# Differential attention: where the normalized head outputs are kept, and how many bias tiles there are

## The chip, the cores and the metric

One core of a Trainium2 chip runs one launch of the kernel. The metric is the device time of a launch in microseconds; the times shown are the median of three runs and the time of one further, profiled execution. The core has five engines that run side by side and wait for each other by semaphores: TensorE (PE; its weight loads are shown as PEld), VectorE (DVE), ScalarE (ACT), GpSimd (POOL) and SyncE (SP), which here issues nearly all DMA transfers, in order, from one queue.

## The reference, cut to what matters

The model is a decoder trunk of two layers over 256 tokens of width 2048 in float32. Layer 0 mixes tokens by gated linear attention, layer 1 by differential attention; each is followed by a SwiGLU block. The change lies in layer 1, in the part below, which is done for 8 heads of size 128 with values of size 256:

```
scores = einsum('bhmqd,bhmkd->bhmqk', qb, k_sh)          # m = 0, 1: two score maps per head
scores = scores + bias                                   # T5 bias by distance, one table per head
scores = where(dist >= 0, scores, -inf)
p = softmax(scores, axis=-1)
a = p[:, :, 0] - lam * p[:, :, 1]
o = einsum('bhqk,bhke->bhqe', a, v_sh)
...
o = rmsnorm(o, subln_g) * (1.0 - lambda_init)
return o.reshape(b, s, D_MODEL) @ w_out
```

The queries are taken in two blocks of 128, called b = 0 and b = 1 here. By causality block 0 sees 128 keys and block 1 sees 256.

## The kernel before, in words

Every large product is made from weights that stream through one ring of buffers: SP loads 512 KB of weights into a `raw` tile (line 223, five buffers), ACT casts it to a high part `hi` (line 238, nine buffers), DVE makes the rest `lo` (line 241), and TensorE multiplies with both. A product that wants the result transposed is made in blocks by `block_w` (line 429): 32 matmuls (lines 438, 439) accumulate one PSUM tile `acc`, and its two halves are added by way of a scratch tile: ACT copies one half to it (line 450), DVE adds (line 451). `scratch()` (line 187) gives tiles of 128x512 from one tag `hs` with three buffers.

The stage of the change begins when the keys are made and goes on into the output product. For each head h two blocks of `diff_w_q` give q(h), DVE scales it (line 1121), and `diff_stages` (line 954) is called. It loads the head's bias tile by SP (line 959) and puts six steps on a list with due times; `tick()` counts them down, once in the middle and once at the end of the first half of a block, once in the middle of its second half, and once after each block. One head is eight ticks long. The steps and their ticks:

- 3, `scores`: for each block b, two matmuls of q with the keys (line 968), DVE adds the bias into the score tile s0 or s1 (line 972), DVE takes the maximum (line 976), ACT makes the exponentials in place (line 978).
- 6, `combine`: DVE makes a = p0 - lam p1 in place (lines 985 to 990).
- 9, `a_T`: PE transposes the three 128x128 pieces of a (line 998, one of b = 0 and two of b = 1), ACT copies them to the tile aT (line 1000).
- 11, `att_v`: six matmuls of aT with the values into two acc tiles (line 1007), ACT takes their squares (line 483).
- 13, `normed`: DVE, POOL (line 478) and DVE normalize (line 1019); the result is called og.
- 14, `out_T`: four transposes of og (line 1028), ACT and DVE write the high and low part to diff_oT (lines 1031, 1032).

So the last steps of head h fall into the time of head h+1. In the order of the program `scores` of head h+1 (its tick 3, which is tick 11 of head h) comes before `normed` and `out_T` of head h. Score tiles have one buffer for each b: s1 of head h+1 is written in the place of s1 of head h, and has to wait for the last use of it. Before the change og lies in that place: `normed` writes both blocks' og over s1 of its own head, and `out_T` reads it from there:

```
og = ctx["s"][1][0][:, b, :]
```

After head 7 `proj_out` follows (line 827): the product of diff_oT with `diff_w_out` (lines 302 to 304), in four column chunks; the step s of a chunk needs diff_oT of head s. The steps of heads 6 and 7 that are still due fall into its first chunk.

A planner puts the instructions of each engine in order before the launch: it follows the program's order as priority, plays the program through on times of its own, and takes what is ready. The order that the engines then run is fixed, and each engine takes its instructions in that order.

Of the kernel before, what the change touches and what calls it, by code (L numbers as in the profile page):

```python
# [11 lines left out]
F32 = mybir.dt.float32  # L12
# [6 lines left out]
P = 128  # L19
D = 2048  # L20
SEQ = 256
# [130 lines left out]
class Trunk:  # L152
# [801 lines left out]
    def diff_stages(self, dp, oT, q, kT, v, h):  # L954
        nc = self.nc
        ctx = {}
        bias = dp.tile([P, SEQ], F32, tag="bias", name=f"bias{h}", bufs=2)
        src = self.bias_dram[h]
        nc.sync.dma_start(bias, bass.AP(tensor=src.tensor, offset=src.offset + 127, ap=[[383, P], [1, SEQ]]))

        def scores():
            ctx["s"] = []
            for b in range(2):
                n = P * (b + 1)
                sp = self.acc()
                sp3 = sp[:, : 2 * n].rearrange("p (m k) -> p m k", m=2)
                for m in range(2):
                    nc.tensor.matmul(
                        sp3[:, m, :], q[:, m, b * P : (b + 1) * P], kT[:, 2 * h + m, :n], start=True, stop=True
                    )  # L970
                s = dp.tile([P, 2, n], F32, tag=f"s{b}", name=f"s{h}_{b}")
                nc.vector.tensor_tensor(
                    out=s, in0=sp3, in1=bias[:, None, SEQ - n :].to_broadcast([P, 2, n]), op=ALU.add
                )
                st = self.stat(8)
                nc.vector.tensor_reduce(out=st[:, 0:2], in_=s, axis=AX.X, op=ALU.max, negate=True)
                for m in range(2):
                    nc.scalar.activation(
                        s[:, m, :], s[:, m, :], AF.Exp, bias=st[:, m : m + 1], accum_out=st[:, 2 + m : 3 + m]
                    )  # L980
                ctx["s"].append((s, st))

        def combine():
            for s, st in ctx["s"]:
                nc.vector.reciprocal(st[:, 4:6], st[:, 2:4])
                nc.vector.tensor_tensor(out=st[:, 6:7], in0=st[:, 5:6], in1=self.neg_lam, op=ALU.mult)
                nc.vector.tensor_scalar(
                    out=s[:, 1, :], in0=s[:, 1, :], scalar1=st[:, 6:7], scalar2=None, op0=ALU.mult
                )
                nc.vector.scalar_tensor_tensor(  # L990
                    out=s[:, 0, :], in0=s[:, 0, :], scalar=st[:, 4:5], in1=s[:, 1, :], op0=ALU.mult, op1=ALU.add
                )

        def a_T():
            tpa = self.tp()
            for b, (s, _) in enumerate(ctx["s"]):
                for kb in range(b + 1):
                    nc.tensor.transpose(tpa[:, b + kb, :], s[:, 0, kb * P : (kb + 1) * P], self.ident)
            ctx["aT"] = dp.tile([P, 3, P], F32, tag="aT", name=f"aT{h}")
            nc.scalar.copy(ctx["aT"], tpa[:, :3, :])  # L1000

        def att_v():
            ctx["o"] = []
            for b in range(2):
                o = self.acc()
                for kb in range(b + 1):
                    nc.tensor.matmul(  # L1007
                        o[:, :SEQ], ctx["aT"][:, b + kb, :], v[:, kb, h * SEQ : (h + 1) * SEQ],
                        start=(kb == 0), stop=(kb == b),
                    )  # L1010
                ss = self.stat()
                self.square(o[:, :SEQ], ss[:, 0:1])
                ctx["o"].append((o, ss))

        def normed():
            ctx["og"] = []
            for b, (o, ss) in enumerate(ctx["o"]):
                og = ctx["s"][1][0][:, b, :]
                nc.vector.scalar_tensor_tensor(
                    out=og, in0=o[:, :SEQ], scalar=self.rstd(ss, SEQ, 1), in1=self.subg, op0=ALU.mult, op1=ALU.mult  # L1020
                )
                ctx["og"].append(og)

        def out_T():
            tpo = self.tp()
            for b in range(2):
                for j in range(2):
                    nc.tensor.transpose(tpo[:, 2 * j + b, :], ctx["og"][b][:, j * P : (j + 1) * P], self.ident)
            hi, lo = (oT.part(2 * h, 2, slice(None), i) for i in range(2))
            tpo2 = tpo.rearrange("p (j b) t -> p j (b t)", j=2)  # L1030
            nc.scalar.copy(hi, tpo2)
            nc.vector.tensor_tensor(out=lo, in0=tpo2, in1=hi.bitcast(F32), op=ALU.subtract)

        for subs, fn in ((3, scores), (6, combine), (9, a_T), (11, att_v), (13, normed), (14, out_T)):
            self.defer(subs, fn)
# [201 lines left out]
```

## Time and profile before

| | |
|---|---|
| median of three runs | 2243.23 us (2242.36 to 2243.86) |
| the profiled execution: its time | 2241.63 us |
| its span, first to last instruction | 2239.9 us |
| mean granted TensorE clock | 0.999 of full speed |
| PE, PEld, DVE, ACT busy | 99%, 82%, 72%, 52% of the span |
| DMA | 438 MB, 196 GB/s over the span |
| the stage of the change, from the first `scores` to the last `out_T` | 1318.9 to 1458 us of the span |

The profile is of one execution. A wait is shown with the engine and line that ended it. Times in the rows are microseconds from the first instruction, and durations of a group are nanoseconds of one instruction where the row gives a mean.

### The profile page before, as it was taken

The numbers are of one execution on the slowest core, as the hardware profiler recorded it, in microseconds if no ns is written. First come the engines' busy times: TensorE is split into PE (matmuls) and PEld (weight loads), VectorE is DVE, ScalarE is ACT, GpSimd is POOL, SyncE is SP. The second block draws the span as 40 slices with busy tenths as digits, with TensorE's granted clock in tenths as the row PEclk, the third lists the DMA queues.
The fourth block names the chain that finished last, engine by engine and source line by source line (L and its number), as shares of the span: only waits on it lengthen the run. The fifth ranks groups of instructions, "written<-read, shape, count | busy, mean of one in ns | idle before, by whom it ended". The sixth has DMA issues, their size and how long they took to land.

```text
span 2239.9 us, 28021 instructions
## 1 busy us (share of the span) xinstructions
PE 2210.2 (99%) x10310; PEld 1835.3 (82%) x10310; DVE 1605.4 (72%) x2093; ACT 1166.4 (52%) x1602; POOL 38.9 (2%) x68
## 2 busy tenths in 40 slices
PE   8999999999999999999999999999999999999998
PEld 7887888888888888888788887788888888888886
DVE  7865554986885886787665567649868858867975
ACT  8654444755553554455565455447555535544552
POOL 2000000000000000000000000000000000000000
PEclk9999999999999999999999999999999999999999
DMA  8555555665565556566665554465655655565573
GB/s 299 168 174 180 176 175 188 213 225 198 201 220 181 186 192 223 170 206 258 208 206 179 188 175 147 163 183 209 228 179 197 217 178 197 192 216 172 200 254 103
DMA packets 123135, 438.37 MB, mean 196 GB/s; under 512 B 13883, under 2 KB 16612, under 8 KB 121460
## 3 DMA queue, kind: packets, MB, share of 16 engines
q1 hardware_dynamic: 121964, 434.99, 57.9%
q8 instruction: 81, 1.33, 0.2%
q10 hardware_dynamic: 1032, 1.57, 0.2%
q14 instruction: 58, 0.48, 0.1%
HBM read 428.11 MB, written 9.97 MB: 196 GB/s over the span
## 4 chain that ended last, share of the span: by engine, by line
PE 97%; DVE 1%; ACT 1%; issue 1%; DMA 0%; POOL 0%; SPq 0%; DVEq 0%; POOLq 0%; ACTq 0%
PE acc L304 14%; PE acc L302 14%; PE acc L303 14%; PE acc L347 12%; PE acc L345 12%; PE acc L346 12%; PE acc L438 8%; PE acc L439 4%; PE tp L459 1%; PE tp L494 1%; PE tp L347 1%; PE tp L345 1%; PE tp L346 1%; PE acc L1007 1%; DVE lo L241 0%
## 5 line engine op out<-in xcount | busy, mean ns | idle before, releaser
L241 DVE TENSOR_TENSOR lo<-raw,hi 128x1024 fp32r<-128x1024 f32 x842 | 1013.7, 1223 | 513.1 <-ACT hi L238 509.7
L238 ACT CAST hi<-raw 128x1024 fp32r<-128x1024 f32 x846 | 873.4, 1052 | 830.6 <-PE acc L304 375.5
L346 PE MATMUL acc<-lo,h_ffn 128*128 128x512 f32 x780 | 304.3, 390 | 0.0
L347 PE MATMUL acc<-hi,h_ffn 128*128 128x512 f32 x780 | 304.1, 390 | 0.0
L345 PE MATMUL acc<-hi,h_ffn 128*128 128x512 f32 x780 | 303.9, 390 | 0.0
L302 PE MATMUL acc<-hi,f_ffn_gT 128*128 128x512 f32 x704 | 274.8, 390 | 0.0
L303 PE MATMUL acc<-lo,f_ffn_gT 128*128 128x512 f32 x704 | 274.1, 389 | 0.0
L304 PE MATMUL acc<-hi,f_ffn_gT 128*128 128x512 f32 x704 | 272.1, 389 | 0.0
L345 PEld LDWEIGHTS acc<-hi,h_ffn 128*128 128x128 f32 x780 | 146.4, 188 | 30.5
L347 PEld LDWEIGHTS acc<-hi,h_ffn 128*128 128x128 f32 x780 | 146.5, 188 | 30.4
L346 PEld LDWEIGHTS acc<-lo,h_ffn 128*128 128x128 f32 x780 | 146.5, 188 | 30.2
L302 PEld LDWEIGHTS acc<-hi,f_ffn_gT 128*128 128x128 f32 x704 | 132.2, 188 | 27.8 <-issue 0.6
L304 PEld LDWEIGHTS acc<-hi,f_ffn_gT 128*128 128x128 f32 x704 | 132.2, 188 | 27.4
L303 PEld LDWEIGHTS acc<-lo,f_ffn_gT 128*128 128x128 f32 x704 | 132.2, 188 | 27.1
L302 PE MATMUL acc<-hi,h_mix 128*128 128x512 f32 x256 | 102.1, 400 | 0.0
L347 PE MATMUL acc<-hi,f_ffn_forms 128*128 128x512 f32 x260 | 101.8, 392 | 0.0
L345 PE MATMUL acc<-hi,f_ffn_forms 128*128 128x512 f32 x260 | 101.8, 392 | 0.0
L346 PE MATMUL acc<-lo,f_ffn_forms 128*128 128x512 f32 x260 | 101.2, 389 | 0.0
L303 PE MATMUL acc<-lo,h_mix 128*128 128x512 f32 x256 | 100.3, 392 | 0.0
L304 PE MATMUL acc<-hi,h_mix 128*128 128x512 f32 x256 | 100.1, 392 | 0.0
L438 PE MATMUL acc<-h_mix,hi 128*128 128x512 f32 x272 | 96.7, 400 | 0.0
L438 PE MATMUL acc<-h_q,hi 128*128 128x512 f32 x256 | 93.2, 405 | 0.0
(227 smaller groups left out, 3351.0 us busy)
## 6 DMA issues: line engine op xcount, KB each, us to landing
raw<-in_w_gu_dram SPq DMA_DIRECT2D x352, 512.0 KB, 4.6
raw<-in_w_d_dram SPq DMA_DIRECT2D x176, 512.0 KB, 4.4
raw<-in_gla_w_r_dram SPq DMA_DIRECT2D x32, 512.0 KB, 3.6
raw<-in_gla_w_v_dram SPq DMA_DIRECT2D x32, 512.0 KB, 3.6
raw<-in_gla_w_out_dram SPq DMA_DIRECT2D x32, 512.0 KB, 3.6
raw<-in_w_v_dram SPq DMA_DIRECT2D x32, 512.0 KB, 4.4
raw<-in_w_k_dram SPq DMA_DIRECT2D x32, 512.0 KB, 3.5
raw<-in_diff_w_q_dram SPq DMA_DIRECT2D x32, 512.0 KB, 3.5
```

Source lines behind the costliest of these rows:

```text
L238: nc.scalar.copy(hi, src)
L241: eng.tensor_tensor(out=lo, in0=src, in1=hi.bitcast(F32), op=ALU.subtract)
L302: nc.tensor.matmul(ps, ah, rh, start=(kt == 0), stop=False)
L303: nc.tensor.matmul(ps, ah, rl, start=False, stop=False)
L304: nc.tensor.matmul(ps, al, rh, start=False, stop=(kt == 2 * ns - 1))
L345: nc.tensor.matmul(ps, ah, wh, start=first, stop=False)
L346: nc.tensor.matmul(ps, ah, wl, start=False, stop=False)
L347: nc.tensor.matmul(ps, al, wh, start=False, stop=last)
L438: nc.tensor.matmul(ps, lh, aT.both(kt), start=(kt == 0), stop=False)
L439: nc.tensor.matmul(ps[:, SEQ:], ll, aT.hi(kt), start=False, stop=(kt == KT - 1))
L459: nc.tensor.transpose(tp[:, j, :], src[:, j * P : (j + 1) * P], self.ident)
L494: nc.tensor.transpose(tp[:, j, :], xc[:, j * P : (j + 1) * P], self.ident)
```

## The change

Two lines differ. The bias tile of a head gets the pool's one buffer, where it had two. And og of each block is written to a scratch tile of its own (the first 256 of its 512 columns), where it was written over s1. The number of instructions and their sizes stay the same.

```diff
@@ def diff_stages(self, dp, oT, q, kT, v, h):
-        bias = dp.tile([P, SEQ], F32, tag="bias", name=f"bias{h}", bufs=2)
+        bias = dp.tile([P, SEQ], F32, tag="bias", name=f"bias{h}")
...
         def normed():
             ctx["og"] = []
             for b, (o, ss) in enumerate(ctx["o"]):
-                og = ctx["s"][1][0][:, b, :]
+                og = self.scratch()[:, :SEQ]
                 nc.vector.scalar_tensor_tensor(
                     out=og, in0=o[:, :SEQ], scalar=self.rstd(ss, SEQ, 1), in1=self.subg, op0=ALU.mult, op1=ALU.mult
                 )
```

## Rows read from the trace of the kernel before

**Rows 1.** The page: busy time of each engine, and the chain that ended last, by engine.
```profile
PE 2210.2 (99%) x10310; PEld 1835.3 (82%) x10310; DVE 1605.4 (72%) x2093; ACT 1166.4 (52%) x1602; POOL 38.9 (2%) x68
...
PE 97%; DVE 1%; ACT 1%; issue 1%; DMA 0%; POOL 0%; SPq 0%; DVEq 0%; POOLq 0%; ACTq 0%
```

**Rows 2.** Windows: stretch, length, busy PE, PEld, DVE, ACT, POOL (instructions), clock, DMA share, GB/s.
```profile
1318.86:1332.96 14.10, 14.10 (x84) 12.41 (x83) 10.28 (x20) 9.61 (x19) 0.00 (x0) 1.00 0.55 175
1332.96:1349.16 16.20, 14.87 (x86) 12.78 (x85) 13.17 (x27) 9.10 (x23) 1.06 (x2) 1.00 0.48 157
...
1397.87:1414.17 16.30, 14.98 (x87) 12.87 (x86) 11.64 (x24) 8.52 (x20) 1.09 (x2) 1.00 0.46 138
...
1438.19:1462.00 23.81, 20.27 (x95) 16.27 (x94) 13.28 (x26) 10.36 (x23) 2.19 (x4) 1.00 0.56 199
```

**Rows 3.** Waits from 1305 to 1470 us: who for whom, total us, times, longest.
```profile
ACT hi L238 <- PE acc L438: 37.3, 31, 1.8
...
PE acc L1007 <- ACT aT L1000: 7.9, 6, 1.3
...
PE acc L302 <- ACT diff_oT L1031: 1.2, 1, 1.2
...
PE acc L304 <- DVE diff_oT L1032: 1.1, 1, 1.1
```

**Rows 4.** Timeline of PE: start, duration, line, tiles, count, idle time before.
```profile
1346.00 0.44 PE L998 MATMUL tp<-ident,s 128*128 128x128 f32 x2
1347.76 1.56 PE L1007 MATMUL acc<-v_sh,aT 128*128 128x256 f32 x6 [1.33 <-ACT aT L1000]
...
1353.94 0.38 PE L1028 MATMUL tp<-ident,s 128*128 128x128 f32 x2
```

**Rows 5.** Timeline of ACT over the same head.
```profile
1346.01 1.04 ACT L238 CAST hi<-raw 128x1024 fp32r<-128x1024 f32 x1 [1.72 <-PE acc L438]
1346.96 0.36 ACT L450 COPY hs<-acc 128x256 f32<-128x256 f32 x1
1347.23 0.48 ACT L1000 COPY aT<-tp 128x384 f32<-128x384 f32 x1
...
1357.53 0.36 ACT L450 COPY hs<-acc 128x256 f32<-128x256 f32 x1
```

**Rows 6.** Timeline of DVE over the same head.
```profile
1339.76 0.69 DVE L972 TENSOR_TENSOR s<-acc,bias 128x512 f32<-128x512 f32 x1 [0.33 <-PE tp L1028]
...
1345.47 0.48 DVE L990 SCALAR_TENSOR_TENSOR s<-s,st 128x256 f32<-128x256 f32 x1
...
1351.07 0.47 DVE L1019 SCALAR_TENSOR_TENSOR s<-acc,st,subg 128x256 f32<-128x256 f32 x1
```

**Rows 7.** Timelines of DVE, PE and ACT for head 0.
```profile
1321.76 0.68 DVE L972 TENSOR_TENSOR s<-acc,bias 128x512 f32<-128x512 f32 x1
...
1326.03 0.49 DVE L990 SCALAR_TENSOR_TENSOR s<-s,st 128x256 f32<-128x256 f32 x1
...
1330.27 0.38 PE L998 MATMUL tp<-ident,s 128*128 128x128 f32 x2
...
1331.66 1.46 PE L1007 MATMUL acc<-v_sh,aT 128*128 128x256 f32 x6
...
1330.68 0.48 ACT L1000 COPY aT<-tp 128x384 f32<-128x384 f32 x1 [0.93 <-PE tp L998]
```

**Rows 8.** Timeline of PE at the end of the stage (heads 6 and 7).
```profile
1442.67 0.50 PE L302 MATMUL acc<-hi,diff_oT 128*128 128x512 f32 x1 [1.18 <-ACT diff_oT L1031]
...
1445.05 0.50 PE L304 MATMUL acc<-hi,diff_oT 128*128 128x512 f32 x1 [1.07 <-DVE diff_oT L1032]
...
1448.68 1.56 PE L1007 MATMUL acc<-v_sh,aT 128*128 128x256 f32 x6 [1.29 <-ACT aT L1000]
```

**Rows 9.** Timeline of SP, and the bias tile's time from issue to landing.
```profile
1340.48 0.33 SPq L959 DMA_DIRECT2D bias<-bias_dram  x1
...
DMA to landing us min/median/max: 2.5/3.1/3.6
```

## The prediction, made before the result was known

> **What bounds the kernel now.** I read the page first: PE is busy 99% of the span, and 97% of the chain that ended last lies on it [rows 1]. So the time is PE's own work plus the gaps in which it stands still, and of an edit that changes no instruction of PE only the gaps matter: 2239.9 - 2210.2 = 29.7 us in the whole span. The next view is a table of windows from one head's scores to the next head's [rows 2], to see which gaps lie where the change is. Between the scores of heads 0 and 1 PE has no gap (14.10 of 14.10 us). From then on each head takes 16.2 to 16.3 us, of which PE is busy 14.9: a gap of 1.33 us for 16.20 - 14.87, of 1.32 for the last of five such windows. The stretch at the end, where heads 6 and 7 run into the output product, has a gap of 23.81 - 20.27 = 3.54 us. The list of waits names them [rows 3]: six waits of the att_v matmuls for ACT's copy of aT, 7.9 us in all, and one each of the output product for the high and the low part of diff_oT, 1.2 and 1.1 us. Together 10.2 us. The chance of the change is therefore between 0 and about 10 us of 2241.63, whatever else it moves.
>
> The third view is the order on the three engines round one of the gaps. On PE the two transposes of block b = 1 stand directly ahead of att_v [rows 4]: they start at 1346.00, and att_v starts at 1347.76 after 1.33 us of waiting, because ACT has a weight cast and a half copy in front of the aT copy [rows 5]. The transposes are that late because a of b = 1 is just then ready: the last DVE instruction on it runs from 1345.47 to 1345.95 [rows 6]. And that chain began late: the bias add of b = 1 started at 1339.76, and what ended DVE's wait in front of it is line 1028, the transposes of the og of the head before [rows 6]. Its scores begin at 1332.96, where a window of [rows 2] begins, 6.8 us earlier: they lie in PSUM because s1 is still og's place. This closes a ring: og of head h holds s1; s1 holds the scores of h+1; these hold att_v of h+1, and this its og.
>
> Head 0 shows the stage without the ring, since nobody holds s1 ahead of it. Its add of b = 1 starts at 1321.76, 2.9 us after its scores begin at 1318.86, and a is ready at 1326.52. The two transposes run at 1330.27, the copy to aT ends at 1331.16, and att_v at 1331.66 has no wait [rows 2, 7].
>
> **The change part by part.** *og in scratch.* The same 16 instructions write as many elements and the same 32 transposes read them; this part costs nothing, and nothing below it, as PE's busy time and DVE's are the same. What it removes is the wait of the b = 1 add for line 1028. For heads 1 to 7 the add can then start as soon as DVE has served the work of b = 0. In head 0 this took 2.9 us from the scores; there, however, DVE had no normalization of an earlier head to do (10.28 us of work in its window against 11.6 to 13.2 later [rows 2]). If I allow the whole difference of up to 2.9 us, the add starts 5.8 us after the scores begin, so at about 1338.8, and if it is served as in head 0, at 1335.9: 1 to 4 us earlier than 1339.76. The chain from add to a takes 6.2 us now (1339.76 to 1345.95) and 4.8 in head 0. So a would be ready between 1335.9 + 4.8 = 1340.7 and 1338.8 + 6.2 = 1345.0, that is 1.0 to 5.3 us earlier than now. To take away the gap whole it has to be early enough for the copy: from the start of the transposes to the end of the aT copy is 0.9 us where ACT is free, as in head 0 (1330.27 to 1331.16), and 1.7 where a cast is in front (1346.00 to 1347.71). Att_v could come without a gap at 1346.00 + 0.44; so the need is 0.5 to 1.3 us, and the middle of the gain, 3 us, is well above it. Value taken: the five gaps in heads 1 to 5 go, 1.33 + 3 x 1.32 + 1.32, about 6.6 us, less 1.0 for two heads in which the copy still stands close ahead (2 x 0.5). Bounds: 0 to 6.6.
>
> *The end of the stage.* Head 7's att_v waits 1.29 us in the same way, and the output product waits 1.18 and 1.07 us because out_T of head 6 stands directly ahead of the product's step that needs it [rows 8]. Both follow from att_v of head 6 being late, which follows from its s1. I take all 3.5 us; bounds 0 to 3.5.
>
> *What is late next.* With the gaps gone PE is busy throughout, as between heads 0 and 1. The weights do not come next: ACT's casts wait 37.3 us for PE to free a `hi` tile [rows 3], so they stand ready ahead of PE. Nor does out_T of head h: og's last instruction ends at 1351.54 and its transposes start at 1353.94, 2.4 us later [rows 4, 6].
>
> *Scratch tiles.* Three buffers now serve two og and the half copies of the q blocks. An og pair would be held from about 1350 until out_T, whose first pair of transposes starts at 1353.94; the next half copy is at 1357.53, 3.6 us behind that [rows 4, 5]. The half copy before it starts at 1346.96, and its reader on DVE is done before og is written. I take 0. If that cover went, ACT would stand still behind the half copy, with casts and the aT copy queued behind it; as long as out_T comes in its 3.6 us, nobody waits.
>
> *One bias tile.* The load of a head waits now for the adds of the head two before it; afterwards it waits for those of the head before. Today's load is issued at 1340.48, 0.03 us after the b = 1 add ended (1339.76 + 0.69) [rows 6, 9]. Issued at that very time under the new rule, it is needed only by the add that follows the scores behind att_v at 1347.76 [rows 4], at least 7.3 us later, and it lands in 3.6 at most [rows 9]. At least 3.7 us are left, more if the add comes earlier. On SP the weight loads stand behind it, and they wait for free buffers anyway, as the casts do. Value: 0. If the cover were gone, a landing of 3.1 us would be added per head.
>
> The Trainium skill ("Trainium Kernel Development and Optimization", section Best Practices) asks for double buffers so that transfers lie beside compute; this edit does the contrary. By that rule the seven loads behind the first would show, at 7 x 3.1 = 21.7 us. The row's 7.3 us against 3.6 speaks against it, and it stands among the rivals.
>
> **Sum.** 6.6 - 1.0 + 3.5 = 9.1 us less. The profiled execution took 2241.63 us, so 2232.5 on its scale; it lies 1.6 us under the median of 2243.23, and on the median's scale the time is 2234.1.
>
> **The rivals.**
> 1. *The gap stays at its place, smaller.* The planner may again put the two transposes directly ahead of att_v, since DVE has more to do per head than in head 0 and the planner's times are not the chip's. For it: five heads in a row show just this order. Against it: the add has 1 to 4 us more. Then a gap of 0.5 (ACT free) to 1.33 us (cast in front) stays, 0.9 in the middle: 5 x 0.4 = 2.1 us saved, and half of the end's, 1.8: 2239.3.
> 2. *The change frees nothing.* s1 could be held by something else until as late. For it: nothing in the rows but that DVE's add is also queued behind a weight split. Against: the only other late reader of s1 is line 998, done at 1330.65 in head 0, before the next scores begin at 1332.96 [rows 2, 7]. Time 2243.2.
> 3. *Slower: the freed work pushes og back.* DVE runs in order. If the work of b = 1 is put in front of the normalization of the head before, og is late, and PE waits at out_T, which stands in the middle of a block. The room is 2.4 us; the whole of head 0's chain in front takes 4.76, which leaves a wait of 2.36 us in each of seven heads, 16.5 us against 10.2 saved: 2249.5. It decides for slower beyond 2.4 + 10.2/7 = 3.9 us put in front. Against it: the adds belong in front, but the rest of the chain waits for ACT, and og is ready to be served in that time.
> 4. *Bias late* (the double buffer missed): 21.7 - 9.1 = 12.6 us more, 2255.8. It needs SP to hold the load 3.7 us longer than now.
> 5. *More than the gaps.* The new order also closes gaps nearby (29.7 us exist in all, most far from here): 2 to 5 us more, about 2230.
>
> **How the numbers follow.** Chances: forecast 0.50 (2231.5 to 2237), rival 1 0.25, rival 2 0.07, rival 3 0.07, rival 4 0.04, rival 5 0.07. A difference of 0.2%, 4.5 us, is about what a measurement of this kernel can tell from none. Faster by more: forecast, rival 5 and two fifths of rival 1, which straddles 2238.7: 0.67. Within: the rest of rival 1 and rival 2: 0.22. Slower: rivals 3 and 4: 0.11. The range goes from 2231.0 to 2243.5 and leaves out most of rivals 3, 4 and 5.
>
> **What would show it.** Right: windows of about 14.9 us per head with PE busy throughout; line 1007 gone from PE's waits; the b = 1 add no longer ended by line 1028 and close behind the b = 0 add; the b = 1 transposes some pairs of matmuls ahead of att_v; bias loads issued once per head right after an add. Wrong: line 998 and line 1007 still neighbours with a wait between (rival 1); waits of PE at line 1028 for line 1019 (rival 3); DVE's line 972 waiting for a DMA (rival 4). A change in PE's busy time, or waits outside 1319 to 1462 us, would mean that the planner's new order acts elsewhere, and that my sum is not the whole.

## The result, and the profile after

The changed kernel takes 2229.72 us (median of four runs, 2229.0 to 2229.85), the one before 2242.8 us (median of four): 13.1 us less, ratio 0.994 with a 95% interval of 0.9923 to 0.9958. The direction was forecast, the size was not: 2234.1 us had been predicted, and the time lies under the low end of the range, 2231.0.

The page of the changed kernel first, to be read beside [rows 1]. PE, DVE, ACT and POOL have as many counted instructions as before (the total of 28028 was 28021; it takes in other kinds); the span is 12.1 us shorter. PE's busy time, which the change was not to touch, fell as well, by 1.9 us.

```profile
span 2227.8 us, 28028 instructions
...
PE 2208.3 (99%) x10310; PEld 1835.7 (82%) x10310; DVE 1601.3 (72%) x2093; ACT 1165.2 (52%) x1602; POOL 39.1 (2%) x68
```

PE's waits over the whole span of the changed kernel (who for whom, total, times, longest). PE's three entries in [rows 3] are gone; what is left lies at the launch and in other stages.

```profile
PE tp L494 <- DMA x_in<-in_x_dram: 6.7, 2, 4.4
PE acc L304 <- DVE h_kv L500: 3.5, 2, 2.2
PE acc L304 <- DVE h_ffn L500: 0.6, 2, 0.3
```

The windows from one head's scores to the next head's, as [rows 2] shows them for the kernel before. PE is busy in the whole of each. Heads 1 to 5 took 16.20 to 16.30 us each and take 14.50 to 14.57 now.

```profile
1319.64:1333.74 14.10, 14.10 (x84) 12.40 (x83) 10.27 (x20) 9.60 (x19) 0.00 (x0) 1.00 0.55 172
1333.74:1348.24 14.50, 14.50 (x87) 12.78 (x86) 11.26 (x25) 8.31 (x22) 1.06 (x2) 1.00 0.46 152
...
1362.81:1377.32 14.51, 14.51 (x87) 12.81 (x86) 11.27 (x25) 8.32 (x22) 1.06 (x2) 1.00 0.52 152
...
1406.40:1423.86 17.46, 17.46 (x92) 14.75 (x91) 12.60 (x26) 9.52 (x23) 1.06 (x2) 1.00 0.52 158
1423.86:1449.90 26.04, 26.04 (x124) 21.64 (x123) 16.73 (x30) 12.51 (x27) 2.12 (x4) 1.00 0.69 239
```

These rows also say where the time came from. From the scores of head 1 to those of head 6 it was 1414.17 - 1332.96 = 81.21 us and is 1406.40 - 1333.74 = 72.66: 8.55 us less over five heads, 1.71 a head. From the scores of head 6 to the end it was 2239.9 - 1414.17 = 825.73 and is 2227.8 - 1406.40 = 821.40: 4.33 less. Together 12.9 us. Ahead of the stage this one profile is 0.78 us longer (1319.64 for 1318.86); the profiles of the experiments begin the stage anywhere from 1318.3 to 1320.2, so that is spread.

The timeline of DVE in the changed kernel, from head 3 on, against [rows 6]:

```profile
1364.21 0.41 DVE L972 TENSOR_TENSOR s<-acc,bias 128x256 f32<-128x256 f32 x1
...
1364.60 0.68 DVE L972 TENSOR_TENSOR s<-acc,bias 128x512 f32<-128x512 f32 x1
...
1366.51 0.47 DVE L1019 SCALAR_TENSOR_TENSOR hs<-acc,st,subg 128x256 f32<-128x256 f32 x1
...
1368.66 0.48 DVE L990 SCALAR_TENSOR_TENSOR s<-s,st 128x256 f32<-128x256 f32 x1
```

The two adds stand side by side, with one short instruction between them. The one of b = 1 starts 1.8 us after the scores (1364.60 against 1362.81) and waits for nothing; before it started 6.8 us after them. The attention a of b = 1 is ready 6.3 us after the scores (1369.14), before it was 13.0. On PE the transposes now lie well ahead of att_v (to be read against [rows 4]):

```profile
1357.99 0.38 PE L998 MATMUL tp<-ident,s 128*128 128x128 f32 x2
1358.13 0.36 PE L439 MATMUL acc<-h_q,lo 128*128 128x256 f32 x1
...
1361.51 1.46 PE L1007 MATMUL acc<-v_sh,aT 128*128 128x256 f32 x6
...
1369.56 0.38 PE L1028 MATMUL tp<-ident,hs 128*128 128x128 f32 x2
...
1422.57 1.46 PE L1007 MATMUL acc<-v_sh,aT 128*128 128x256 f32 x6
```

3.5 us lie between the transposes and att_v, and PE fills them with the matmuls of the next q block. Out_T at 1369.56 comes 2.6 us after og is ready at 1366.98, so nobody waits there either. SP and the time of the bias loads, against [rows 9]:

```profile
1365.31 0.33 SPq L959 DMA_DIRECT2D bias<-bias_dram  x1
...
DMA to landing us min/median/max: 3.0/3.1/3.9
```

The load is issued 0.03 us after the b = 1 add has ended, once per head, and lands at the latest 3.9 us later; the next head's scores begin at 1377.32, 12.0 us behind the issue. This is so in every steady head; ahead of head 1 it is 10.5 us (1323.25 to 1333.74). SP itself does stand still ahead of these loads, 7.8 us in six waits for DVE, where it was 1.7 us in five before. PE shows nothing of that.

### The profile page after: what moved, and what is told of

Read it like the earlier page. It is cut to its first block, busy times and chain, and to the rows that moved or that the text cites. A ratio compares the mean times of both kernels' runs of the same rounds, so it can differ in the third digit from the quotient of the medians.

```text
span 2227.8 us, 28028 instructions
## 1 busy us (share of the span) xinstructions
PE 2208.3 (99%) x10310; PEld 1835.7 (82%) x10310; DVE 1601.3 (72%) x2093; ACT 1165.2 (52%) x1602; POOL 39.1 (2%) x68
## 3 DMA queue, kind: packets, MB, share of 16 engines
q8 instruction: 81, 1.33, 0.2%
## 4 chain that ended last, share of the span: by engine, by line
PE 97%; DVE 1%; issue 0%; DMA 0%; ACT 0%; POOL 0%; SPq 0%; DVEq 0%; POOLq 0%; ACTq 0%
PE acc L304 15%; PE acc L302 15%; PE acc L303 15%; PE acc L347 12%; PE acc L345 12%; PE acc L346 12%; PE acc L438 8%; PE acc L439 4%; PE tp L459 1%; PE tp L494 1%; PE tp L347 1%; PE tp L345 1%; PE tp L346 1%; PE acc L968 0%; PE acc L1007 0%
```

## The experiments

Each was timed beside the kernel before on the same chip; ratios are to it, with a 95% interval.

**The two edits apart.** In the first kernel only og moves:

```diff
-                og = ctx["s"][1][0][:, b, :]
+                og = self.scratch()[:, :SEQ]
```

> Only og goes to scratch tiles; the bias keeps two tiles. Ring theory (og over s1 closes a ring from the out_T transposes of a head to the bias add of the next; the bias tile has no part): 2229.7 us as the whole change, att_v without waits. Rival (the second bias tile gone has its own effect, by the order of loads on SP): between 2229.7 and 2242.8, or faster than 2229.7, by over 1 us.

Measured: 2229.21 us, ratio 0.9943 (0.993 to 0.9956). In the second only the bias tile changes:

```diff
-        bias = dp.tile([P, SEQ], F32, tag="bias", name=f"bias{h}", bufs=2)
+        bias = dp.tile([P, SEQ], F32, tag="bias", name=f"bias{h}")
```

> Only the bias tile goes from two buffers to one; og stays over s1. Ring theory: 2242.8 us, six waits of att_v for aT, 7.9 us, as before. Rival (bias order matters): off 2242.8 by over 1 us. Rule of double buffers: slower by up to 21.7 us.

Measured: 2242.04 us, ratio 1.0 (0.9991 to 1.0008). PE's waits for aT are gone in the first (none is left in the stage) and as before in the second (six, 8.0 us). So the gain is og's. The bias edit shows no effect: the medians lie 0.3 us apart, and the interval is about 2 us wide to either side.

**The loads of the bias tile.** Seven of the eight are taken out of the changed kernel.

```diff
-        bias = dp.tile([P, SEQ], F32, tag="bias", name=f"bias{h}")
+        if h == 0:
+            self.bias0 = dp.tile([P, SEQ], F32, tag="bias", name="bias0")
+        bias = self.bias0
         src = self.bias_dram[h]
-        nc.sync.dma_start(bias, ...)
+        if h == 0:
+            nc.sync.dma_start(bias, ...)
```

> As the changed kernel, but the bias tile of head 0 is loaded once and used by all heads (seven loads are left out, so heads 1 to 7 compute with the wrong table). If the seven loads are hidden: 2229.7 us. If waits for the one bias tile cost anything: faster, by up to 1 us for each load that shows.

Measured: 2230.4 us, ratio 0.9943 (0.9929 to 0.9956), the same as with the loads within the spread. PE waits for nothing in the stage in either kernel: the loads are hidden. The Trainium skill ("Trainium Kernel Development and Optimization", section Best Practices) asks for double buffers; here one buffer is enough, since 12.0 us lie between the issue and the next scores, and 3.9 are needed.

**og in a third place.** The query tile of a head is dead once its scores are made.

```diff
-                og = self.scratch()[:, :SEQ]
+                og = q[:, b, :]
```

> og of head h is written over the query tile of head h (two buffers, dead after the scores), neither to scratch nor over s1; one bias tile. Ring theory: s1 is free after its transposes, so 2229.7 us and no waits of att_v, whatever place og has. Rival (the scratch tiles themselves bring the gain): 2242.8. It could lose if q of head h+2 has to wait for out_T of head h: then DVE's line 451 shows that wait.

Measured: 2229.13 us, ratio 0.994 (0.9928 to 0.9953). PE has no wait in the stage, so the gain has nothing to do with scratch tiles. The wait that was feared is there, in the list of waits from 1305 to 1470 us of this kernel, and costs PE nothing:

```profile
DVE q L451 <- PE tp L1028: 3.1, 6, 0.5
```

**Half of og, and the other score tile.** First only og of b = 0 leaves s1:

```diff
-                og = self.scratch()[:, :SEQ]
+                og = ctx["s"][1][0][:, 1, :] if b else self.scratch()[:, :SEQ]
```

> og of b = 0 goes to scratch, og of b = 1 stays over its half of s1; one bias tile. Ring theory: s1 is held as long as before, 2242.8 us, and the b = 1 add still waits for line 1028. Rival (each og moved brings its share): about 2236.

Measured: 2241.89 us, ratio 0.9999 (0.999 to 1.0008). Half the traffic moved and nothing gained; the b = 1 add waits for the transposes of og as in [rows 6]:

```profile
1339.48 0.69 DVE L972 TENSOR_TENSOR s<-acc,bias 128x512 f32<-128x512 f32 x1 [0.33 <-PE tp L1028]
```

Then s1 is left free, and s0 is held instead:

```diff
-                og = self.scratch()[:, :SEQ]
+                og = self.scratch()[:, :SEQ] if b else ctx["s"][0][0].rearrange("p m k -> p (m k)")
```

> og of b = 0 is written over s0, og of b = 1 goes to scratch; one bias tile. s1 is free early, s0 is held to out_T. Ring theory: the ring closes through s0; all three transposes stand ahead of att_v again. The chain of b = 0 is shorter (adds of 0.42 for 0.68 us and so on), but planner and engines put it in one row with b = 1: 2240 to 2245 us with waits of att_v. Rival (it is the long b = 1 chain alone): 2229.7 to 2232.

Measured: 2241.55 us, ratio 0.9995 (0.9987 to 1.0004). The time is that of the closed ring. In this kernel's timeline of PE all three transposes now stand close ahead of att_v, where in the kernel before the one of b = 0 ran 5 us earlier, and there are two gaps in a row:

```profile
1346.30 0.27 PE L998 MATMUL tp<-ident,s 128*128 128x128 f32 x1
1346.83 0.44 PE L998 MATMUL tp<-ident,s 128*128 128x128 f32 x2 [0.26 <-DVE s L990]
1348.12 1.56 PE L1007 MATMUL acc<-v_sh,aT 128*128 128x256 f32 x6 [0.86 <-ACT aT L1000]
```

DVE's timeline for the next head, whose scores begin at 1349.52, shows the wait at its new place, and how it reaches b = 1:

```profile
1351.57 0.68 DVE L972 TENSOR_TENSOR s<-acc,bias 128x512 f32<-128x512 f32 x1
1354.66 0.42 DVE L972 TENSOR_TENSOR s<-acc,bias 128x256 f32<-128x256 f32 x1 [2.41 <-PE tp L1028]
...
1356.14 1.01 DVE L976 TENSOR_REDUCE st<-s 128x2 f32<-128x256 f32 x2
```

The add of b = 0 waits 2.41 us for line 1028 (12.0 us in five heads). The add of b = 1 comes early, as s1 is free, but its maximum stands behind the late add in DVE's fixed order, so a of b = 1 is late all the same, 13.4 us after the scores. Through s0 the ring therefore needs the planner's order as well as the buffer; why the planner put the maximum there is not shown.

**How much one gap costs.** The heads are divided: og of heads 0 to 3 goes to scratch and that of heads 4 to 7 stays over s1, and the other way round.

```diff
-                og = self.scratch()[:, :SEQ]
+                og = self.scratch()[:, :SEQ] if h < 4 else ctx["s"][1][0][:, b, :]
```

> og of heads 0 to 3 goes to scratch, og of heads 4 to 7 stays over s1; one bias tile. This opens the ring for heads 1 to 4 and leaves the gaps of head 5 and of the end. Theory A (a gap costs what the distance of the scores showed, 1.63 to 1.77 us a head): 6.8 us saved, 2236.0. Theory B (a gap costs its idle time alone, 1.33 us, and the rest of the 13.1 us comes from elsewhere): 5.3 saved, 2237.5. Theory C (the planner's new order comes as a whole): 2229.7 or 2242.8.

> og of heads 4 to 7 goes to scratch, og of heads 0 to 3 stays over s1; one bias tile. Gaps of heads 1 to 4 stay, head 5 and the end are freed. Theory A: 13.1 - 6.8 = 6.3 us saved, 2236.5, and the two halves add up to the whole. Theory B: 1.33 + 3.5 = 4.9 saved, 2237.9. Theory C: 2229.7 or 2242.8.

Measured: 2235.82 us (ratio 0.9971, 0.996 to 0.9981) and, with h >= 4 in the condition, 2236.02 us (0.9973, 0.9963 to 0.9984), both beside 2242.3. They save 6.5 and 6.3 us, which adds up to 12.8, so the gain comes head by head and theory C is out. Theory A forecast 6.8 and 6.3; idle time alone would have given 5.3 and 4.9. The medians lie near theory A, but the intervals, 4.3 to 9.0 and 3.6 to 8.3 us, hold both, so the totals do not decide. Two neighbouring windows of the first kernel do, within one run: head 4, freed, and head 5, not freed (columns as in [rows 2]).

```profile
1376.60:1391.11 14.51, 14.51 (x86) 12.80 (x85) 11.27 (x25) 8.33 (x21) 1.06 (x2) 1.00 0.46 149
1391.11:1407.41 16.30, 14.92 (x86) 12.83 (x85) 13.21 (x27) 9.11 (x23) 1.06 (x2) 1.00 0.49 168
```

The difference is 1.79 us. Only 16.30 - 14.92 = 1.38 of it is idle time of PE; the other 0.41 is in its busy time, for the same matmuls.

**A shorter gap.** The ring stays closed, but the copy to aT is moved from ACT, where a cast is in front of it, to DVE; and the same is done to the changed kernel, as a control.

```diff
-            nc.scalar.copy(ctx["aT"], tpa[:, :3, :])
+            nc.vector.tensor_copy(ctx["aT"], tpa[:, :3, :])
```

> The kernel before (ring closed), but the copy to aT is made by DVE, where it follows the last instruction on a directly and has no cast in front of it. The ring stays; each gap gets shorter: from 1.33 us to about 0.6 (0.44 of the transposes is PE's own time, the copy takes about 0.5). Theory A (a gap costs its idle time and some 0.35 us in which PE runs empty though it counts as busy): six gaps x 0.7 = 4.2 us saved, 2238.1, and what is left over the changed kernel, 8.5 us, is more than the 6 us of idle left. Theory B (idle time alone, the rest from the planner's order): the excess over 2229.7 equals the idle time left, about 6 us, 2235.7.

> The changed kernel (ring open) with the same copy on DVE. If a copy's engine matters only where a gap is: 2229.3 us as the changed kernel, no waits of att_v. If DVE's load is near its limit (0.5 us more per head): slower by up to 8 x 0.5 = 4 us.

Measured: 2238.53 us (ratio 0.9982, 0.9973 to 0.9991) with the ring closed, 2229.66 us (0.9942, 0.9928 to 0.9955) with it open, where PE has no wait in the stage and the copy's engine makes no difference to the time. With the ring closed 4.25 us are saved, as theory A forecast (4.2); theory B's 2235.7 lies outside the interval. What is left over the open kernel is 8.9 us, though PE's waits in the stage have only 6.1 us left. In the first kernel a steady head and its gap look like this:

```profile
1364.10:1379.66 15.56, 14.91 (x87) 12.83 (x85) 12.11 (x26) 8.15 (x19) 1.09 (x2) 1.00 0.46 145
```

```profile
1346.02 0.44 PE L998 MATMUL tp<-ident,s 128*128 128x128 f32 x2
1347.11 1.56 PE L1007 MATMUL acc<-v_sh,aT 128*128 128x256 f32 x6 [0.65 <-DVE aT L1000]
```

The gap is 0.65 us of idle time instead of 1.33, and the head takes 15.56 us, 1.05 more than an open one at 14.51. So beside the idle time 0.40 us stay; with the gap of 1.33 it is 16.20 - 14.50 - 1.33 = 0.37. The share is nearly the same at both lengths, so it is a price of each such gap, not of its length. Where it arises can be seen in the rows. A matmul's shown time overlaps that of the next, and idle time counts only from where the last shown time ends: the two transposes ahead of the gap take 0.44 us of busy time, though in a stream the next matmul starts 0.14 after them (1357.99 and 1358.13 in the changed kernel), and the six matmuls behind the gap take 1.56 for 1.46. That is 0.30 + 0.10 us, close to the 0.37 to 0.41 of the windows.

## Why the prediction was wrong, point by point

*The mechanism was right.* The ring from og over s1 to the next head's add was named as the cause, and the runs bear it out wherever they test it: og's place alone decides (2229.21 us), half of it does nothing (2241.89), a third place serves as well (2229.13), and the time of the closed ring comes back with og over s0 (2241.55). One thing the prediction read too simply: the wait of the b = 1 add for line 1028 is recorded for head 1 alone (0.3 us). In heads 2 to 6 the add stands behind a weight split in DVE's order and starts 0.6 to 0.7 us after the transposes have ended. So the ring acts mostly through the order that the planner fixed because of it, and little of it is seen as a wait. All eight waits of PE went, and nothing came in their place.

*The failed step is the price of a gap.* "The five gaps in heads 1 to 5 go, 1.33 + 3 x 1.32 + 1.32, about 6.6 us, less 1.0", and 3.5 us at the end: sum 9.1. Two terms were mis-sized.

- The gaps were priced at the idle time that the waits and the windows show. Measured, the five heads gave 8.55 us where 6.6 of idle time went, and the end 4.33 for 3.5. The missing 2.7 us stood in the windows before as busy time of PE: 14.87 to 14.98 us a head, for work that takes 14.50 to 14.57 without the gap. The text took "busy" for work ("PE's own work plus the gaps in which it stands still"), and so put the upper bound of the gain at 10 us, and expected windows of 14.9 us. The Trainium skill ("Perfetto Trace Analysis", section Identifying the Most-Contended Engine) says that the busy share of matmuls is not a good measure of how close a kernel is to roofline, because pipelined instructions look smaller in the trace. This trace agrees that the busy time is no measure of the work: the same matmuls count as 14.87 us with a gap and as 14.50 without.
- The 1.0 us kept back for copies that would stand close ahead of att_v was not needed: the transposes came 3.5 us ahead of it.

9.1 + 1.0 + 2.7 = 12.8, against 13.1 between the medians. The 1.0 us alone would have left the forecast at 2233.1, inside the range; the 2.7 us took the time out of it.

*The add of b = 1* was forecast 2.9 to 5.8 us behind the start of the scores and came at 1.8; the rows of head 0, with a weight split and a half sum between the two adds, were a poor measure of it. a was forecast 1.0 to 5.3 us earlier and came 6.7 earlier. This helped, but what it gave beyond closing the gap is worth nothing.

*The end of the stage* was taken whole, as forecast, and by the path forecast: att_v of head 6 comes 16.2 us after its scores (the last row of the changed kernel's PE timeline, 1422.57, against 1406.40); before it was 22.7 (1436.90 against 1414.17), by this row of the kernel before:

```profile
1436.90 1.46 PE L1007 MATMUL acc<-v_sh,aT 128*128 128x256 f32 x6
```

*Scratch tiles and the bias tile* were put at 0 each: right. The half copies do not appear among the waits, and the bias loads have 8 us to spare in a steady head (6.6 ahead of head 1) where at least 3.7 were forecast.

*The rivals.* Rival 2 fell with the result. Rival 1, a smaller gap at the same place, did not come. Rival 3, og pushed back, was near in order but not in time: both adds and both maxima do stand in front of the last L1019, and the room up to out_T is still 2.6 us. Rival 4 is refuted by the two bias runs. Rival 5 came nearest in time, but its reason, gaps closed elsewhere, is not what happened: PE's waits outside the stage are as before within 0.2 us each (6.9, 3.4 and 0.6 us before). That its 2230 came out is chance. The sign given for such a case, a change in PE's busy time, did come; it lay in the stage itself, at the gaps, and did not mean that the order acted elsewhere.

## What to carry to other kernels

A tile that is used again for a late result of the same item keeps its first user of the next item waiting; ask for each reuse who is next in that place, and whether the late user hangs on that one by a chain, since then it closes a ring. Price a gap of TensorE by the distance between starts of the same instruction with and without the gap (16.2 and 14.5 us here), and not by the idle time alone (1.33): each gap of a steady head had another 0.37 to 0.41 us that the profile counts as busy. The second buffer for a load was worth nothing here, where the time from the last use to the next need (10.5 to 12.0 us) is longer than the landing (at most 3.9).

## What had not been expected of the hardware

That the extra price of a gap is so constant in the steady heads: 0.37 us with 1.33 of idle time, 0.40 with 0.65. At the end of the stage it was less: 4.33 - 3.54 = 0.79 us for three gaps, which was not taken apart. Where two gaps followed each other (og of b = 0 over s0) a steady head took 16.22 us with 15.10 busy by its window:

```profile
1365.69:1381.91 16.22, 15.10 (x87) 12.87 (x85) 11.46 (x24) 8.42 (x20) 1.09 (x2) 1.00 0.42 139
```

This is 0.6 us of busy time more than the 14.51 of an open head, with only 1.1 of idle time. That the second gap brings its own share fits, but was not taken apart further.
